# Early weights for the first three ConvFFN units, and one page of w_o a block, in a decoder-layer kernel

## The chip, the cores and the metric

The kernel runs on one core of a Trainium2 chip (one launch, no other core busy). The metric is the device time of that core in microseconds (us), the median over several runs. Five engines are named as in the profile: PE is TensorE (PEld its weight loads), DVE is VectorE, ACT is ScalarE, POOL is GpSimd, SP is SyncE, which here only issues DMAs. Each engine runs its own instructions strictly in the order in which they stand; an instruction that has to wait holds up all that stands behind it on its engine.

## The reference, cut to what matters

The layer takes x (1024 rows of 1024 channels). Three token mixers (stick-breaking attention, mLSTM, cross-attention) and their gates come first and are not touched. What matters here is the end of the merge, the output projection, and the ConvFFN:

```
merged = (gates[:, :, 0] * (y_sb @ w_sb_out[l])
          + gates[:, :, 1] * (y_ml @ w_ml_out[l])
          + gates[:, :, 2] * (y_xa @ w_xa_out[l]))
x = x + merged @ w_o[l]

h = _rmsnorm(x, g_ffn[l])
u = _causal_dwconv(h @ w_up[l], ff_conv_w[l], ff_conv_b[l])
u_val, u_gate = jnp.split(u, 2, axis=-1)
x = x + (jax.nn.silu(u_gate) * u_val) @ w_down[l]
```

w_up is 1024 x 5632: 22 tiles of 128 columns for u_val and 22 for u_gate. All is float32.

## The kernel before, in words

**A matmul is three passes.** Every float32 operand is split into a rounded part and a rest: ACT copies the rounded part (L129), DVE subtracts it from the value (L130). `mm3` (L141 to L144) then multiplies part by part: L142 rounded by rounded, L143 rounded weight by rest of the input, L144 rest of the weight by rounded input.

**Large products have seven parts in place of eight.** Two row halves (l, u) by two halves of the inner dimension (a, b) by two column tiles are computed with seven products of sums and differences (Strassen's scheme in Winograd's form). The output projection does it in seven stages (`stage`, L1224, called from L1235 on); the sums of w_o's pages that it needs are made by `wo_sums` (L1086), a generator stepped once a block (L1141 calls `next(beside)`) while the branches' output projections run, in the last 16 of those 24 blocks. It loads eight pages of 512 KB, two a step, and then does one DVE operation a step (L1096).

**A ConvFFN unit** (`seven`, L698) makes one column tile f of u_val and one of u_gate. Its weights are four quarters: a1, b1 (u_val, first and second half of the inner dimension) and a2, b2 (u_gate). It needs s1 = a2 + b2, a difference a1 - a2, s2 = s1 - a1 (`sums`, L691: DVE operations L694, L695, L696) and b1 - s2 (L727). Its products, 12 matmuls each, are: a1 by "au" and b1 by "bu" (first stage), s2 by "t2" and the difference by "t3" (second stage), s1 by "t1" (third), b1 - s2 by "bl" and b2 by "t4" (fourth). A `yield` ends each stage; the code at the end of the projection steps three units (`first`) by hand and then the others in turn. Inputs au and bu (rows' upper half) are there first; t2 and t3, t1, bl and t4 depend on the norm of the lower half and are split later by ACT and DVE (L1204, L1357, L1366, L1372 and L129, L130).

**Weights of a product** go through two rings, whi and wlo, of two buffers each, so a buffer is free when the product before the last one has been done. `qring` splits a loaded quarter (ACT, DVE). `qadd`, used for the raw quarters a1, b1, b2 of units 0 to 3, spares DVE: ACT makes the rounded part (L671) and its negative (L672), and a DMA issued by POOL adds the weight from DRAM to the negative (L673).

**Order.** A scheduler places the instructions of each engine when the program is built, from the code's order, priorities (`tc.high_priority`) and its own model of times. Before the change only unit 0's weights (L1272 to L1276) are loaded, summed and (a1 alone) split beside the projection's fifth stage. Units 1 and 2 load theirs inside `seven`; their sums stand in DVE's order after the first stages of all three units.

Of the kernel before, what the change touches and what calls it, by code (L numbers as in the profile page):

```python
# [28 lines left out]
NF = DFF // P  # L29
# [13 lines left out]
def tile_hybrid_layer(ctx: ExitStack, tc: tile.TileContext, xT, memT, vecs, w_t, w_n, w_kv, w_if,  # L43
# [4 lines left out]
    nc = tc.nc  # L48
# [19 lines left out]
    def T(shape, tag, dt=F32, bufs=None):  # L68
        pool = {"mw": mlp, "mst": mlp, "px": late[0], "sx": late[0]}.get(tag, sb)
        return pool.tile(shape, dt, tag=tag, name=nm(tag), bufs=bufs or BUFS[tag])  # L70
# [4 lines left out]
    def half(dt=F32):  # L75
        return T([P, HALF], "hf", dt)

    def wide():
        return T([P, S], "U")
# [22 lines left out]
    def hs(h):  # L102
        return slice(h * HALF, (h + 1) * HALF)

    def ts(t):
        return slice(t * P, (t + 1) * P)
# [19 lines left out]
    SOON, LEAD = 40, 60  # L126

    def split(src, hi, lo, eng=None):
        nc.scalar.activation(hi, src, AF.Copy)  # L129
        (eng or nc.vector).tensor_sub(lo, src, hi.bitcast(F32))  # L130
# [10 lines left out]
    def mm3(out, lh, ll, rh, rl, start, stop, more=False):  # L141
        nc.tensor.matmul(out, lh, rh, start=start, stop=False, skip_group_check=more)  # L142
        nc.tensor.matmul(out, lh, rl, start=False, stop=False, skip_group_check=more)  # L143
        return nc.tensor.matmul(out, ll, rh, start=False, stop=stop, skip_group_check=more)  # L144
# [317 lines left out]
    R = NCH * MLH  # L462
# [69 lines left out]
    early = []  # L532
    for b in range(2):
        raw = T([P, S], "y")
# [3 lines left out]
    first = chunks((1,))  # L538
# [110 lines left out]
    RAWS = [itertools.chain(("raw", "raw", "pg"), itertools.repeat("raw")), itertools.repeat("pg")]  # L649

    def turn(i, tags):
        cyc[i] += 1
        return tags[cyc[i] % len(tags)]

    def pair(tag):
        t = T([P, 2, HALF], tag, F32R)
        return t[:, 0], t[:, 1]
# [4 lines left out]
    def qring(src, soon=SOON):  # L662
        t = pair(turn(0, ("whi", "wlo")))
        with tc.high_priority(offset=soon):
            split(src, *t)
        return t

    def qadd(src, dram, soon=SOON):
        t = pair(turn(0, ("whi", "wlo")))
        with tc.high_priority(offset=soon):  # L670
            nc.scalar.activation(t[0], src, AF.Copy)  # L671
            nc.scalar.activation(t[1], t[0].bitcast(F32), AF.Copy, scale=-1.0)  # L672
            nc.gpsimd.dma_start(t[1], dram, accum_op=ALU.add)  # L673
        return t

    def prod(p, a, b, start=True):
        for k in range(4):
            mm3(p, a[0][:, ts(k)], a[1][:, ts(k)], *b[k], start and k == 0, k == 3, not start)

    def halves(src, tag):  # L680

        if tag == "me":
            t = [T([P, HALF], tag) for _ in range(2)]
            for i in range(2):
                nc.sync.dma_start(t[i], src[:, hs(i)])
            return t
        r = T([P, S], tag)
        nc.sync.dma_start(r, src)
        return r[:, hs(0)], r[:, hs(1)]

    def sums(w, s1, s2):  # L691

        a1, b1, a2, b2 = w
        nc.vector.tensor_add(s1, a2, b2)  # L694
        nc.vector.tensor_sub(a2, a1, a2)  # L695
        nc.vector.tensor_sub(s2, s1, a1)  # L696

    def seven(w1, w2, x, done, ready=None, adds=False, pause=False):  # L698

        def raw(src, w, i):  # L700
            return qadd(src, w[:, hs(i)], LEAD) if adds else qring(src)

        w, s1, s2, hl1 = ready or ((*halves(w1, next(RAWS[0])), *halves(w2, next(RAWS[1]))), None, None, None)
        a1, b1, a2, b2 = w
        L, p2 = bank(turn(2, LONG)), bank(turn(3, SHORT))
        prod(L, hl1 or raw(a1, w1, 0), x["au"])
        c1 = wide()
        up, lo = c1[:, hs(1)], c1[:, hs(0)]
        nc.scalar.activation(up, L, AF.Copy)
        if pause:  # L710
            yield
        prod(p2, raw(b1, w1, 1), x["bu"])
        nc.vector.tensor_add(up, up, p2)
        if not ready:
            s1, s2 = half(), a1
            sums(w, s1, s2)
        yield
        prod(L, qring(s2, 1000 if ready else SOON), x["t2"], False)
        c2 = wide()
        nc.scalar.activation(c2[:, hs(1)], L, AF.Copy)  # L720
        R = bank(turn(3, SHORT))
        prod(R, qring(a2, 1000 if ready else SOON), x["t3"])
        yield
        prod(L, qring(s1), x["t1"], False)
        nc.scalar.activation(c2[:, hs(0)], L, AF.Copy)
        nc.vector.tensor_add(c2[:, hs(0)], c2[:, hs(0)], R)
        nc.vector.tensor_sub(b1, b1, s2)  # L727
        yield
        prod(L, qring(b1), x["bl"], False)
        nc.scalar.activation(lo, L, AF.Copy)  # L730
        done(0, c1)
        prod(R, raw(b2, w2, 1), x["t4"], False)
        nc.vector.tensor_add(c2[:, hs(1)], c2[:, hs(1)], R)  # L733
        done(1, c2)
        yield

    def middle(u):
        next(u)
        next(u)
# [338 lines left out]
    def wo_load(q, i, j, tag):  # L1078
        t = T([P, S], tag)
        n = 4 * i + 2 * j  # L1080
        nc.sync.dma_start(t.rearrange("p (n c) -> p n c", n=2), w_o[n:n + 2, :, hs(q)].rearrange("n p c -> p n c"))
        return t
# [3 lines left out]
    def wo_sums():  # L1086
        raw = []
        for j in range(2):
            for qi in (((0, 0), (0, 1)), ((1, 1), (1, 0))):
                raw += [wo_load(q, i, j, "pg") for q, i in qi]  # L1090
                yield
        for j in range(2):
            a1, a2, b2, b1 = raw[4 * j:4 * j + 4]
            for i, op, out, x, y in ((2, nc.vector.tensor_sub, a2, a1, a2), (1, nc.vector.tensor_sub, b2, b2, a2),
                                     (0, nc.vector.tensor_add, a1, a1, b2), (3, nc.vector.tensor_sub, b1, b1, b2)):
                op(out, x, y)  # L1096
                ws[i][j] = out
                yield

    def fine(src, *tags):  # L1100
        t = [T([P, S], tag, F32R) for tag in (tags[0], tags[-1])]
# [13 lines left out]
    w1 = []  # L1115
    beside = wo_sums()
    for i in range(3 * KT):
        b, n = i // KT, ORDER[i % KT]
        if n == 0:
            ys = [branch(b, j) for j in range(4)]  # L1120
        if n < 4:
            raw = T([P, S], "raw")
# [4 lines left out]
        for h in (1, 0):  # L1127
# [4 lines left out]
            dst, t = block(n, h), th[:, hs(h)]  # L1132
# [50 lines left out]
    def grow(o, banks, d):  # L1183
        nc.vector.scalar_tensor_tensor(part(o, d), banks[d], 0.5, part(o, d), op0=ALU.mult, op1=ALU.add)
# [29 lines left out]
    L, R = four(SHORT), four(LONG)  # L1214
# [33 lines left out]
    R = four(LONG)  # L1248
# [23 lines left out]
    w = (*halves(w_up[0], "me"), *halves(w_up[NF], "h"))  # L1272
    early = w, T([P, HALF], "sx"), wide()[:, :HALF]
    sums(*early)
    early += (pair("U"),)
    split(w[0], *early[3])  # L1276

    o1l = out_tiles(0, 0, "y")
    diff = [page("h") for _ in range(2)]
# [6 lines left out]
    def after6(d):  # L1286
        if d == 1:
            with tc.issue_after(last[0].ins):
                upper["r"] = rstd(acc[1], HALF)
        if d == 3:  # L1290
            with tc.issue_after(last[0].ins):
                pr = spread(upper["r"], 4)
            upper["rows"] = half()
            nc.scalar.activation(upper["rows"], pr, AF.Copy)
        grow(o2l, L, d)
        squares(0, part(o2l, d))
        nc.scalar.activation(part(blg, d), part(o2l, d), AF.Copy, scale=col(C_GFFN + 4 + d))
        if d % 2:
            keep(o2l, 1, 0, d // 2)
# [22 lines left out]
    def ffn_up(f):  # L1322
        ys = {}

        def done(g, c):
            i = g * NF + f
            ys[g] = y = T([P, S], "y")
            conv(c, [col(C_FW + 3 * i + 2 - s) for s in range(3)], col(C_FB + i), y)
            if g:
                nc.scalar.activation(y, y, AF.Silu)  # L1330
                nc.vector.tensor_mul(ys[0], ys[0], y)
                if f // 2 == 5:
                    nc.sync.dma_start(act_d[5, f % 2], ys[0])
                else:
                    nc.sync.dma_start(act_d[f // 2, :, :, hs(f % 2)].rearrange("h p r -> p h r"),
                                      ys[0].rearrange("p (h r) -> p h r", h=2))

        return seven(w_up[f], w_up[NF + f], fx, done, early if f == 0 else None, f < 4, f < 3)


    fd, fx = {}, {"au": bau, "bu": bbu}
    for n, tags in (("t2", ("h",)), ("t3", ("pg",)), ("t1", ("h",)), ("bl", ("pg",)), ("t4", ("h", "pg"))):
        fd[n], fx[n] = doubles(*tags)
    units = [ffn_up(f) for f in range(NF)]
    first = units[:3]
    cyc[2], cyc[3] = 1, 1
    next(first[0])
# [6 lines left out]
    with tc.high_priority(offset=300):  # L1354
# [3 lines left out]
            split(full[j], *fd["t2"][j])  # L1358
        for j in range(2):
            split(diff[j], *fd["t3"][j])  # L1360
    for u in first[:2]:
        next(u)
    for j in range(2):
        bl = x1p[2 + j]
# [7 lines left out]
        nc.vector.tensor_sub(full[2 + j], full[2 + j], full[j])  # L1372
        split(full[2 + j], *fd["t4"][j])
    next(first[0])
    middle(first[2])
    next(first[1])
    last = first[2]
    for u in units[3:]:
# [70 lines left out]
    R = [bank(turn(2, LONG)) for _ in range(4)]  # L1449
    L = [bank(turn(3, SHORT)) for _ in range(4)]  # L1450
    au, al, bu, bl, wc = [], [], [], [], []
# [167 lines left out]
```

## Time and profile before

| | |
|---|---|
| runs | 1638.05 us median of 3 (1635.67 to 1638.61) |
| the profiled execution | 1639.59 us; span from first to last instruction 1637.9 us |
| granted TensorE clock, mean | 0.998 |
| PE busy | 99% of the span, 7959 matmuls |
| DVE, ACT, POOL busy | 75%, 51%, 6% |
| DMA | mean 131 GB/s |

The lists of rows below and in the prediction come from this profile. In a timeline row the columns are start (us), duration, engine, line, operation, output<-inputs, shapes, how many were merged, and in brackets the idle time before it with what ended it. A busy PE is not a PE at its peak, since matmuls are pipelined: one starts 0.23 us after the one before it and lasts 0.39 us. What tells is a larger step between starts. The branches' output projections end near 917 us, the output projection of w_o runs to 994 us, and the ConvFFN's units start there.

### The profile page before, as it was taken

The page shows a single profiled execution, that of the slowest core. Times are in us where ns is not written, and L with a number is a line of the kernel's source. Part 1 is how long each engine was busy: PE and PEld are TensorE (multiplying, and loading weights), DVE is VectorE, ACT ScalarE, POOL GpSimd, SP SyncE. Part 2 cuts the span into 40 slices and gives each one's busy share as a digit, 9 for nine tenths or more (in the row PEclk, how much of TensorE's full clock was granted, in tenths as well). Part 3 has the DMA queues.
Part 4 walks back from the last instruction along what each step waited for, and adds up shares of the span by engine and source line. Part 5 has one row for each costly group of instructions (what it writes and reads, how often), then busy time and mean ns, then how long its engine had stood idle before and what let it go on. Part 6 is the DMA issues. An engine that isn't in the chain of part 4 may idle for free.

```text
span 1637.9 us, 21193 instructions
## 1 busy us (share of the span) xinstructions
PE 1617.3 (99%) x7959; PEld 1322.9 (81%) x7959; DVE 1225.8 (75%) x1674; ACT 835.1 (51%) x1281; POOL 104.4 (6%) x175
## 2 busy tenths in 40 slices
PE   8999999999999999999999999999999999999999
PEld 4878888888878888888778887788888888888887
DVE  5658888859774776776576979987787777789864
ACT  4557777645554544666311445655555545543431
POOL 1022222020000110100000001100000000000000
PEclk9999999999999999999999999999999999999999
DMA  8420111324324565434884324431222221577131
GB/s 295 159 66 20 40 40 65 142 95 151 128 99 154 192 191 158 140 111 155 310 293 147 117 97 109 129 103 71 77 82 99 91 78 52 186 303 244 46 135 71
DMA packets 101794, 214.54 MB, mean 131 GB/s; under 512 B 13304, under 2 KB 37176, under 8 KB 101692
## 3 DMA queue, kind: packets, MB, share of 16 engines
q1 hardware_dynamic: 100108, 210.30, 37.0%
q0 software_dynamic: 1584, 2.88, 1.1%
q8 instruction: 63, 1.03, 0.3%
q14 instruction: 39, 0.32, 0.1%
HBM read 158.54 MB, written 54.61 MB: 130 GB/s over the span
## 4 chain that ended last, share of the span: by engine, by line
PE 93%; DMA 2%; DVE 2%; ACT 2%; issue 1%; POOL 0%; SPq 0%; DVEq 0%; ACTq 0%; POOLq 0%
PE ps_pj L142 13%; PE ps_pj L144 13%; PE ps_pj L143 13%; PE ps_pv L144 6%; PE ps_pv L142 6%; PE ps_pv L143 6%; PE ps_tr L142 4%; PE ps_tr L143 4%; PE ps_tr L144 4%; PE ps_z L142 4%; PE ps_z L144 4%; PE ps_z L143 4%; PE ps_pv L440 2%; PE ps_tr L420 2%; PE ps_z L395 1%; PE ps_z L394 1%
## 5 line engine op out<-in xcount | busy, mean ns | idle before, releaser
L143 PE MATMUL ps_pj<-h,whi 128*128 128x512 f32 x520 | 204.1, 393 | 0.0
L142 PE MATMUL ps_pj<-h,whi 128*128 128x512 f32 x440 | 176.4, 401 | 4.0 <-ACT h L129 2.7
L129 ACT ACTIVATE whi<-raw 128x512 fp32r<-128x512 f32 (+1 forms) x99 | 81.2, 821 | 168.7 <-PE ps_pj L143 76.5
L144 PE MATMUL ps_pj<-h,wlo 128*128 128x512 f32 x352 | 137.4, 390 | 0.1
L842 DVE SCALAR_TENSOR_TENSOR y<-U,vec,y 128x1023 f32<-128x1023 f32 x88 | 112.4, 1279 | 8.1 <-ACT y L840 8.1
L143 PEld LDWEIGHTS ps_pj<-h,whi 128*128 128x128 f32 x520 | 98.3, 189 | 20.0 <-DVE h L130 0.8
L408 DVE TENSOR_TENSOR_SCAN U<-U 128x512 f32<-128x512 f32 (+3 forms) x96 | 92.8, 1008 | 22.0 <-POOL U L403 20.4
L142 PE MATMUL ps_pj<-pg,whi 128*128 128x512 f32 x268 | 104.7, 391 | 1.3 <-DVE pg L1134 1.3
L142 PEld LDWEIGHTS ps_pj<-h,whi 128*128 128x128 f32 x440 | 83.2, 189 | 21.8 <-ACT h L129 3.4
L144 PE MATMUL ps_pj<-pg,wlo 128*128 128x512 f32 x248 | 96.7, 390 | 0.0
L144 PEld LDWEIGHTS ps_pj<-h,wlo 128*128 128x128 f32 x352 | 66.1, 188 | 14.7 <-DVE wlo L130 0.6
L129 ACT ACTIVATE whi<-pg 128x512 fp32r<-128x512 f32 (+1 forms) x53 | 43.1, 815 | 66.2 <-PE ps_tr L143 18.3
L143 PE MATMUL ps_pv<-h,whi 128*128 128x512 f32 x190 | 74.0, 389 | 0.0
L143 PE MATMUL ps_pj<-pg,whi 128*128 128x512 f32 x188 | 73.4, 390 | 0.0
L130 DVE TENSOR_TENSOR wlo<-raw,whi 128x1024 fp32r<-128x1024 f32 x44 | 53.7, 1221 | 17.3 <-ACT whi L129 17.3
L840 ACT ACTIVATE y<-U,vec 128x1024 f32<-128x1024 f32 x44 | 54.6, 1242 | 20.6 <-DVE U L733 16.8
L144 PE MATMUL ps_pj<-h,whi 128*128 128x512 f32 x160 | 63.3, 396 | 0.0
L142 PEld LDWEIGHTS ps_pj<-pg,whi 128*128 128x128 f32 x268 | 50.3, 188 | 12.0 <-DVE pg L1134 1.9
L144 PE MATMUL ps_pv<-h,wlo 128*128 128x512 f32 x152 | 59.6, 392 | 0.0
L142 PE MATMUL ps_pv<-h,whi 128*128 128x512 f32 x150 | 58.9, 393 | 0.3 <-DVE U L733 0.3
L130 DVE TENSOR_TENSOR wlo<-raw,wlo 128x512 fp32r<-128x512 f32 x53 | 36.5, 688 | 26.6 <-ACT wlo L129 26.3
L144 PE MATMUL ps_tr<-pg,wlo 128*128 128x512 f32 x144 | 56.0, 389 | 0.0
(489 smaller groups left out, 4478.1 us busy)
## 6 DMA issues: line engine op xcount, KB each, us to landing
raw<-in_w_t_dram SPq DMA_DIRECT2D x29, 512.0 KB
gate_d<-U SPq DMA_DIRECT2D x24, 512.0 KB
U<-gate_d SPq DMA_DIRECT2D x22, 512.0 KB
act_d<-y SPq DMA_DIRECT2D x22, 512.0 KB
pg<-in_w_t_dram SPq DMA_DIRECT2D x21, 512.0 KB
raw<-in_w_dn_dram SPq DMA_DIRECT2D x18, 512.0 KB
h<-act_d SPq DMA_DIRECT2D x14, 512.0 KB
raw<-in_w_br_dram SPq DMA_DIRECT2D x12, 512.0 KB
```

Source lines behind the costliest of these rows:

```text
L129: nc.scalar.activation(hi, src, AF.Copy)
L130: (eng or nc.vector).tensor_sub(lo, src, hi.bitcast(F32))
L142: nc.tensor.matmul(out, lh, rh, start=start, stop=False, skip_group_check=more)
L143: nc.tensor.matmul(out, lh, rl, start=False, stop=False, skip_group_check=more)
L144: return nc.tensor.matmul(out, ll, rh, start=False, stop=stop, skip_group_check=more)
L394: nc.tensor.matmul(z[:, a, :w], qs[a][:, ts(rb)], ks[a][:, c], start=True, stop=False)
L395: nc.tensor.matmul(z[:, a, :w], qs[a][:, ts(rb)], kz[a][:, c], start=False, stop=True)
L408: nc.vector.tensor_tensor_scan(f[:, a, 1:w + 1], f[:, a, 1:w + 1], f[:, a, 1:w + 1], 1.0 if o == 0 else f[:, a, 0:1], op0=ALU.mult, op1=AL ...
L420: nc.tensor.transpose(pt[:, a, ts(j)], g[:, a, ts(j)], ident)
L440: nc.tensor.matmul(pv[64 * a:64 * a + 64, ts(rb % 4)], sbv[s // 2][:, s % 2, (2 * p + a) * 64:(2 * p + a + 1) * 64], wt[a][:, ts(j)], star ...
L840: nc.scalar.activation(out, u, AF.Identity, bias=bias, scale=taps[0])
L842: nc.vector.scalar_tensor_tensor(out[:, :S - s], u[:, s:], taps[s], out[:, :S - s], op0=ALU.mult, op1=ALU.add)
```

## The change

Four things change, all between about 820 and 1065 us:

1. The weights of units 1 and 2 are loaded beside the projection's fifth stage, with unit 0's; their first two sums are made in place in the projection's sixth stage (s1 in b2's place, the difference in a2's), one operation after each of its four column tiles. s2 is made later, in a1's place. So b2 is overwritten, and is loaded a second time (256 KB each, `if s1 is b2`) for the fourth stage.
2. Unit 0's s2 and difference are split there too, into a pair each of the five "U" buffers.
3. Unit 2's second stage is stepped together with those of units 0 and 1, ahead of unit 0's third; before, it came after unit 0's fourth.
4. `wo_sums` loads one page a block in place of two; the subtraction a2 = a1 - a2 shares its step with the operation after it.

```
-        w, s1, s2, hl1 = ready or ((*halves(w1, next(RAWS[0])), *halves(w2, next(RAWS[1]))), None, None, None)
+        w, s1, s2, pre = ready or ((*halves(w1, next(RAWS[0])), *halves(w2, next(RAWS[1]))), None, None, {})
...
-        if not ready:
+        if s1 is None:
             s1, s2 = half(), a1
             sums(w, s1, s2)
+        elif s2 is None:
+            s2 = a1
+            nc.vector.tensor_sub(s2, s1, a1)
...
-        prod(L, qring(s2, 1000 if ready else SOON), x["t2"], False)
+        prod(L, pre.get("s2") or qring(s2), x["t2"], False)
...
+        if s1 is b2:
+            b2 = half()
+            nc.sync.dma_start(b2, w2[:, hs(1)])
...
-            for qi in (((0, 0), (0, 1)), ((1, 1), (1, 0))):
-                raw += [wo_load(q, i, j, "pg") for q, i in qi]
+            for q, i in ((0, 0), (0, 1), (1, 1), (1, 0)):
+                raw.append(wo_load(q, i, j, "pg"))
                 yield
...
+    soon = []
+    for f, tag in ((1, "h"), (2, "pg")):
+        w = (*halves(w_up[f], "raw"), *halves(w_up[NF + f], tag))
+        soon.append((w, w[3], None, {}))
...
+        a1, b1, a2, b2 = soon[d // 2][0]
+        if d % 2 == 0:
+            nc.vector.tensor_add(b2, b2, a2)
+        else:
+            nc.vector.tensor_sub(a2, a1, a2)
...
-    for u in first[:2]:
+    for u in first:
         next(u)
...
     next(first[0])
-    middle(first[2])
+    next(first[2])
     next(first[1])
```

The built order on the engines changes as follows; outside of this stretch it is the same. (Numbers behind a name tell tiles apart; the changed kernel has other line numbers, so L713, L726 and L727 there stand for the same as before or six lines lower.)

**DVE, at the second stages.** First what stood before. raw_8708 and h_8710 are unit 1's weights, raw_8739 and pg_8741 unit 2's; L713 adds up first-stage results; L1204 scales the rows behind "t1", "bl" and "t4", L1366 forms t1.

```order
L713 TENSOR_TENSOR U_8730<-U_8730,ps_z_8713 128x512
L694 TENSOR_TENSOR hf_8797<-h_8710 128x512
L713 TENSOR_TENSOR U_8761<-U_8761,ps_pv_8744 128x512
L695 TENSOR_TENSOR h_8710<-raw_8708,h_8710 128x512
L694 TENSOR_TENSOR hf_8818<-pg_8741 128x512
L696 TENSOR_TENSOR raw_8708<-hf_8797,raw_8708 128x512
L695 TENSOR_TENSOR pg_8741<-raw_8739,pg_8741 128x512
L130 TENSOR_TENSOR wlo_8885<-h_8710,wlo_8885 128x512
L130 TENSOR_TENSOR whi_8867<-raw_8708,whi_8867 128x512
L696 TENSOR_TENSOR raw_8739<-hf_8818,raw_8739 128x512
L130 TENSOR_TENSOR whi_8908<-sx_8462,whi_8908 128x512
L130 TENSOR_TENSOR wlo_8926<-hf_8797,wlo_8926 128x512
```

And now (unit 1: raw_8476, h_8478; unit 2: raw_8480, pg_8482; L1211 is the old L1204, L1385 the old L1366):

```order
L713 TENSOR_TENSOR U_8744<-U_8744,ps_z_8727 128x512
L130 TENSOR_TENSOR whi_8865<-raw_8476,whi_8865 128x512
L130 TENSOR_TENSOR wlo_8883<-h_8478,wlo_8883 128x512
L713 TENSOR_TENSOR U_8771<-U_8771,ps_pv_8754 128x512
L130 TENSOR_TENSOR whi_8898<-raw_8480,whi_8898 128x512
L130 TENSOR_TENSOR wlo_8916<-pg_8482,wlo_8916 128x512
L1211 TENSOR_TENSOR pg_8206<-pg_8206,ps_tr_8751 128x1024
L1211 TENSOR_TENSOR pg_8207<-pg_8207,ps_tr_8751 128x1024
L1385 TENSOR_TENSOR y_8484<-pg_8206,pg_8202 128x1024
```

The six sums are gone from this place: four stand some 45 rows earlier (L1309 and L1311, in the projection's sixth stage), the two that form s2 (L719) some ten rows earlier. Two splits of unit 0's weights have also gone up.

**SP, at the branches' last third.** Before:

```order
L1177 DMA px_8132<-in_xT_dram 128x2x512
L1081 DMA pg_7439<-in_w_o_dram 128x2x512
L1081 DMA pg_7441<-in_w_o_dram 128x2x512
L1081 DMA pg_7475<-in_w_o_dram 128x2x512
L1081 DMA pg_7477<-in_w_o_dram 128x2x512
L1068 DMA U_7515<-gate_d 128x1024
L1081 DMA pg_7517<-in_w_o_dram 128x2x512
L1081 DMA pg_7519<-in_w_o_dram 128x2x512
```

And now:

```order
L1184 DMA px_8132<-in_xT_dram 128x2x512
L1087 DMA pg_7439<-in_w_o_dram 128x2x512
L1087 DMA pg_7473<-in_w_o_dram 128x2x512
L1074 DMA U_7511<-gate_d 128x1024
L1087 DMA pg_7513<-in_w_o_dram 128x2x512
L1087 DMA pg_7547<-in_w_o_dram 128x2x512
L1087 DMA pg_7587<-in_w_o_dram 128x2x512
L1074 DMA U_7545<-gate_d 128x1024
```

The third page of w_o now stands behind a gate page. On DVE the first sum needs pages one and two, the second page three; before, both stood in a row (L1096, L1096); now the rows that empty a PSUM bank and use it (L1143, L1144) stand between them, and the second and third sums stand in a row.

**DVE, beside the projection's sixth stage.** Before:

```order
L696 TENSOR_TENSOR U_8463<-sx_8462,me_8456 128x512
L130 TENSOR_TENSOR U_8467<-me_8456,U_8467 128x512
L1200 TENSOR_TENSOR hf_8031<-hf_8031,hf_8383 128x512
L1184 SCALAR_TENSOR_TENSOR U_8280<-ps_pj_8209,U_8280 128x512
L130 TENSOR_TENSOR wlo_8399<-pg_7439,whi_8398 128x1024
```

And now:

```order
L696 TENSOR_TENSOR U_8463<-sx_8462,me_8456 128x512
L1309 TENSOR_TENSOR h_8478<-h_8478 128x512
L1207 TENSOR_TENSOR hf_8031<-hf_8031,hf_8383 128x512
L1191 SCALAR_TENSOR_TENSOR U_8280<-ps_pj_8209,U_8280 128x512
L130 TENSOR_TENSOR U_8467<-me_8456,U_8467 128x512
L130 TENSOR_TENSOR wlo_8399<-pg_7439,whi_8398 128x1024
```

The first of the four sums has come in; the other three follow in the same way up to the projection's second column tile of that stage.

**PE** changes only within 192 rows, from unit 0's second stage on. The products of 12 matmuls stand there in this order (unit, operand; in brackets those that are interleaved):

```
before: 0 t2, 0 t3, (1 t3 with 1 t2), 0 t1 and 1 t1, (0 bl, 0 t4, 2 t2), 2 t3, (1 bl with 2 t1), 1 t4, 3 au, 3 bu, 2 bl, 2 t4
after:  (0 t2 with 0 t3), 1 t2, 1 t3, 2 t2, 2 t3, 0 t1, 1 t1, 0 bl, 0 t4, 1 bl, (1 t4 with 2 t1), 3 au, (3 bu with 2 bl), 2 t4
```

Before, 36 matmuls stood between the last use of the buffer into which unit 1's b2 (for its "t4") goes and the first use of that b2; after the change, 24 do.

More of the change, by code (lines that the diff above doesn't have):

```diff
@@ L701, in raw @@
             return qadd(src, w[:, hs(i)], LEAD) if adds else qring(src)
-        w, s1, s2, hl1 = ready or ((*halves(w1, next(RAWS[0])), *halves(w2, next(RAWS[1]))), None, None, None)
+        w, s1, s2, pre = ready or ((*halves(w1, next(RAWS[0])), *halves(w2, next(RAWS[1]))), None, None, {})
         a1, b1, a2, b2 = w
         L, p2 = bank(turn(2, LONG)), bank(turn(3, SHORT))
-        prod(L, hl1 or raw(a1, w1, 0), x["au"])
+        prod(L, pre.get("a1") or raw(a1, w1, 0), x["au"])
         c1 = wide()
@@ L721, in seven @@
         R = bank(turn(3, SHORT))
-        prod(R, qring(a2, 1000 if ready else SOON), x["t3"])
+        prod(R, pre.get("a2") or qring(a2), x["t3"])
         yield
+        if s1 is b2:
+            b2 = half()
+            nc.sync.dma_start(b2, w2[:, hs(1)])
         prod(L, qring(s1), x["t1"], False)
@@ L1097, in wo_sums @@
                 ws[i][j] = out
-                yield
+                if i != 2:
+                    yield
     def fine(src, *tags):
@@ L1274, in tile_hybrid_layer @@
     sums(*early)
-    early += (pair("U"),)
-    split(w[0], *early[3])
+    early += ({n: pair("U") for n in ("a1", "s2", "a2")},)
+    for n, t in (("a1", w[0]), ("s2", early[2]), ("a2", w[2])):
+        split(t, *early[3][n])
+    soon = []
+    for f, tag in ((1, "h"), (2, "pg")):
+        w = (*halves(w_up[f], "raw"), *halves(w_up[NF + f], tag))
+        soon.append((w, w[3], None, {}))
     o1l = out_tiles(0, 0, "y")
@@ L1336, in done @@
                                       ys[0].rearrange("p (h r) -> p h r", h=2))
-        return seven(w_up[f], w_up[NF + f], fx, done, early if f == 0 else None, f < 4, f < 3)
+        return seven(w_up[f], w_up[NF + f], fx, done, (early, *soon)[f] if f < 3 else None, f < 4, f < 3)
     fd, fx = {}, {"au": bau, "bu": bbu}
@@ L1344, in tile_hybrid_layer @@
     units = [ffn_up(f) for f in range(NF)]
+    for _ in range(2):
+        next(RAWS[0]), next(RAWS[1])
     first = units[:3]
```

## The prediction

> **What bounds the kernel now.** I read the page first, then TensorE's waits over the whole run, then the stretch where the longest of the late ones lies.
>
> ```profile
> span 1637.9 us, 21193 instructions
> PE 1617.3 (99%) x7959; PEld 1322.9 (81%) x7959; DVE 1225.8 (75%) x1674; ACT 835.1 (51%) x1281; POOL 104.4 (6%) x175
> ```
> ```profile
> PE ps_z L215 <- ACT pg L185: 6.7, 1, 6.7
> PE ps_pj L142 <- ACT h L129: 2.7, 1, 2.7
> PE ps_pj L142 <- DVE U L1136: 1.3, 1, 1.3
> PE ps_pj L142 <- DVE pg L1134: 1.3, 1, 1.3
> ```
>
> TensorE is the bound; only its waits and its clock can be won. The 6.7 us are at the start. Two rows lie where the change works: 2.7 us before the units' "t1" product, and 1.3 us in the branches' projections (L1136). How much the first costs in all is seen in stretches of equal length, the second undisturbed:
>
> ```profile
> core 0: us, PE busy (x) PEld busy (x) DVE busy (x) ACT busy (x) POOL busy (x), PEclk, DMA share, GB/s
> 1012.68:1036.78 24.10, 20.57 (x74) 15.10 (x72) 22.28 (x28) 10.51 (x16) 0.86 (x1) 0.86 0.16 44
> 1080.00:1104.10 24.10, 24.10 (x108) 19.96 (x107) 17.83 (x25) 11.67 (x18) 0.00 (x0) 1.00 0.33 105
> 1027.92:1034.03 6.11, 6.07 (x13) 4.29 (x14) 5.21 (x5) 0.89 (x1) 0.16 (x1) 0.50 0.64 172
> ```
> ```profile
> 1009.96 0.39 PE L142 MATMUL ps_pv<-h,wlo 128*128 128x512 f32 x1
> ...
> 1012.68 0.39 PE L142 MATMUL ps_pj<-h,whi 128*128 128x512 f32 x1
> ```
>
> A product of 12 takes 1012.68 - 1009.96 = 2.72 us, 0.227 a matmul. In the stalled stretch 108 - 74 = 34 matmuls are missing: 34 x 0.227 = 7.7 us. So the 2.7 us row is a third of it. Right behind it TensorE ran 6.11 us at clock 0.50, in which 13 matmuls started that need 2.95 us: 3.2 us lost by the clock. The rest are small waits ahead of the stall.
>
> Why it stalled, from VectorE's timeline and ScalarE's:
>
> ```profile
> 1014.82 0.68 DVE L713 TENSOR_TENSOR U<-U,ps_pv 128x512 f32<-128x512 f32 x1
> 1015.42 0.68 DVE L713 TENSOR_TENSOR U<-U,ps_z 128x512 f32<-128x512 f32 x1
> 1016.01 0.68 DVE L694 TENSOR_TENSOR hf<-h 128x512 f32<-128x512 f32 x1
> ...
> 1022.64 2.34 DVE L1204 TENSOR_TENSOR pg<-pg,ps_tr 128x1024 f32<-128x1024 f32 x2
> 1024.90 2.35 DVE L1366 TENSOR_TENSOR y<-pg,pg 128x1024 f32<-128x1024 f32 x2
> ```
> ```profile
> 1026.82 1.99 ACT L129 ACTIVATE h<-y 128x1024 fp32r<-128x1024 f32 x2
> ```
> ```profile
> 1024.84 0.39 PE L144 MATMUL ps_pv<-pg,wlo 128*128 128x512 f32 x1
> 1027.92 0.79 PE L142 MATMUL ps_pj<-h,whi 128*128 128x512 f32 x1 [2.69 <-ACT h L129]
> ```
>
> VectorE works without a pause there, 0.60 us from start to start at 512 columns (1015.42 to 1016.01) and 1.13 at 1024 (2.26 for two, 1022.64 to 1024.90). The units' sums (L694 on) stand ahead of L1204 and L1366, whose result ScalarE splits for "t1". VectorE's order, not its load over the run, makes the stall.
>
> **The stall, after the change.** I walk the new order with these durations.
> - The six sums are gone from between L713 and L1204; two (the s2's, 1.2 us) now stand about ten rows earlier, and unit 0's two splits (1.2) have gone up altogether. In the same stretch unit 0's b1 - s2 (0.6) has moved behind.
> - With these, the L713 rows start near 1014.0 in place of 1014.82, the L1204 pair at 1018.2 in place of 1022.64, the first L1366 at 1020.5. The first half of "t1" is split by 1024.7, the second by 1026.6.
> - TensorE in the meantime has two products more ahead of "t1" (unit 2's second stage): six from 1012.68, so it asks for "t1" at 1012.68 + 6 x 2.72 = 1029.0. The splits are 2.4 us early even for the last of them. ScalarE's waits for ring buffers (a product earlier each time) are in the walk and leave it ahead.
>
> So the whole 7.7 us go: the idle, the half clock behind it, and the small waits, whose splits (of units 1 and 2) now also come 2 us before use.
>
> **Where the sums went.** Four sums (2.4 us) and two splits (1.2) now lie at 965 to 976. VectorE's pauses there:
>
> ```profile
> 962.65 0.69 DVE L694 TENSOR_TENSOR sx<-h 128x512 f32<-128x512 f32 x1 [0.67 <-DMA h<-in_w_up_dram]
> ...
> 970.11 0.69 DVE L1200 TENSOR_TENSOR hf<-hf,hf 128x512 f32<-128x512 f32 x1 [0.70 <-ACT hf L1199]
> ...
> 976.21 0.69 DVE L1184 SCALAR_TENSOR_TENSOR px<-ps_pv,px 128x512 f32<-128x512 f32 x1 [2.03 <-PE ps_pv L144]
> ```
>
> The walk has VectorE up to 1.2 us late at 974 and level again at 977; the weights it splits there are wanted about 3 us later. Cost nothing, and 1 us for each us if the cover went.
>
> The sums wait for pages. SyncE's issues before:
>
> ```profile
> 958.30 0.35 SPq L688 DMA_DIRECT2D h<-in_w_up_dram  x1
> 962.01 0.33 SPq L688 DMA_DIRECT2D raw<-in_w_up_dram  x1
> 965.89 0.33 SPq L685 DMA_DIRECT2D me<-in_w_up_dram  x1
> 967.10 4.77 SPq L1188 DMA_DIRECT2D x_d<-U  x2
> ```
>
> The page issued at 958.30 was in use at 962.65, 4.35 us later. Unit 1's second page goes right behind it (958.7) and is wanted at 965.2; unit 2's goes behind the first L1188 and one L685 (968.3) and is wanted at 975.3: 7 us. Both fit. Behind a late one on VectorE would stand the statistics of the norm, which TensorE wants at 983. The second load of b2 (two of 256 KB) is issued near 996, in place of a page; nobody wants it before 1037. Cost nothing.
>
> **The new wait.** Unit 1's b2 goes through the adding DMA. Its chain before:
>
> ```profile
> 1046.44 0.62 ACT L671 ACTIVATE whi<-h 128x512 fp32r<-128x512 f32 x1
> 1047.10 0.63 ACT L672 ACTIVATE whi<-whi 128x512 fp32r<-128x512 f32 x1
> ```
> ```profile
> 1048.03 0.86 POOL L673 DMA_DIRECT2D whi<-in_w_up_dram  x1 [19.95 <-PE ps_z L144]
> ```
> ```profile
> DMA to landing us min/median/max: 3.6/6.2/7.2
> ```
>
> L671 to the issue takes 1.6 us, 1.9 with another ScalarE operation between (there is one now), and some 0.4 from TensorE's release. Landing takes L = 3.6 to 7.2. Before, 36 matmuls lay between the buffer's release and its use; now 24, and the third matmul of the product is the first that needs the added part: 27 x 0.227 = 6.1 us after the last matmul that used the buffer. The wait is 2.3 + L - 6.1 = L - 3.8: nought to 3.4 us. Three pages are loaded just ahead of it, so I take L from the upper half, a little under the median: 5.7, and 1.9 us. Behind, unit 3's b1 has 30 matmuls (L - 4.4) and more time once TensorE has waited; unit 2's b2 and unit 0's b2 are within half a microsecond, as unit 1's and 2's were before. Together 2.0 us, bounds 0 and 5.
>
> [...] No adding DMA in this trace landed in under 3.6.
>
> **The pages of w_o.**
>
> ```profile
> 825.19 1.97 SPq L1081 DMA_DIRECT2D pg<-in_w_o_dram  x4
> 830.09 0.34 SPq L1068 DMA_DIRECT2D U<-gate_d  x1
> ```
> ```profile
> 833.94 2.57 DVE L1096 TENSOR_TENSOR pg<-pg,pg 128x1024 f32<-128x1024 f32 x2 [1.42 <-DMA pg<-in_w_o_dram]
> 836.42 0.68 DVE L1136 SCALAR_TENSOR_TENSOR U<-U,ps_pj 128x512 f32<-128x512 f32 x1
> ```
> ```profile
> 837.16 0.50 PE L142 MATMUL ps_pj<-h,whi 128*128 128x512 f32 x1 [1.31 <-DVE U L1136]
> ```
>
> VectorE waited for the second page, did two sums, and only then L1136, which frees TensorE's bank. Now one sum stands ahead of that row: if the page still lands at 833.9, L1136 starts at 835.1 and TensorE at 835.8, so 1.3 us come back. But the third page is now issued behind the gate page, at 830.5. The second page took 8.2 us from 825.7 to use; the third has less ahead of it and I put it at 836.5. Then two sums in a row delay the next bank by 1.0 us. Net gain 0.3; bounds 1.3 gained and, if it also takes 8.2 us (838.7), 3.2 - 1.3 = 1.9 lost and a half clock behind it (3.2).
>
> **Sum.** Gains 7.7 + 0.3, loss 2.0: 6.0 us. Made against the profiled execution (1639.59 us, span 1637.9) that is 1633.6; the median of the runs, 1638.05, is 1.5 lower, so 1632.0.
>
> **Rivals.**
> - *The adding DMAs land early* (3.6 us): no new wait, gain 8.0, 1630.0. For: two before landed that soon, with nothing loaded around them. Against: three pages go ahead now. 0.15.
> - *The new wait halves the clock.* The 2.69 us idle did, the 1.3 us did not; in between no row tells. From L = 6.5 the wait is 2.7 us: 0.8 more than summed, and 3.2 for the clock: 1636.0. For: the median is 6.2. 0.13. [...]
> - *Another late step takes the stall's place*: VectorE is as late as before at another split, gain 1 us, 1637.0. Against: the walk has 2.4 us to spare. 0.06.
> - *Slower: single pages of w_o hold VectorE in block after block.* Place: the four sums that now stand behind a page issued alone (third, sixth, seventh, eighth). It decides from a landing 8 us after issue, as the second page's was: 1.9 us lost at the third page, 2 at each of the others, twice 3.2 for the clock, 14.3 against 7.7 - 2.0 = 5.7 gained: 8.6 slower, 1646.6. Against: less is queued ahead of each than ahead of the second page. 0.06.
> - Forecast: 0.60, its own range 1629 to 1635.
>
> **Numbers.** No change that a measurement can tell is within 0.2%, 3.3 us: 1634.8 to 1641.3. Faster: 0.57 of the forecast, 0.15, and a little of the clock rival: 0.73. Same: the rest of these and the third rival: 0.21. Slower: 0.06. The range goes from the early landing less the runs' spread to the third rival: 1628.5 to 1637.0.
>
> **What would show it.** In the changed profile: no TensorE wait over 1 us between 1010 and 1037 and clock 1.00 there; VectorE's L1204 pair near 1018; a TensorE wait for an adding DMA about 30 us after unit 0's second stage starts; the wait at 837 smaller or one product later. I am wrong if the 2.7 us wait and the clock 0.50 are still in that stretch, if VectorE waits for an in_w_up page near 965 to 976 by over 2 us, or if the branches' stretch lost more than it did.

## The result, and the profile after

| | before | changed |
|---|---|---|
| median, 20 runs each | 1639.24 us (1635.67 to 1642.98) | 1634.67 us (1632.30 to 1638.45) |
| ratio | | 0.9973, 95% interval 0.9965 to 0.9980 |
| profiled execution | 1639.59, span 1637.9 | 1633.01, span 1631.3 |

The median fell by 4.6 us, the profiled execution by 6.6; 6.0 was forecast. One execution of those reported below, of the early sums alone (2), took 2314.81 us at a mean granted clock of 0.655 and is left out of its ratio. The head of the page after the change:

```profile
span 1631.3 us, 21183 instructions
PE 1613.9 (99%) x7959; PEld 1322.4 (81%) x7959; DVE 1226.2 (75%) x1674; ACT 835.5 (51%) x1281; POOL 103.6 (6%) x175
```

VectorE is as busy as before (1226 us): nothing was saved, work was moved. TensorE's waits after the change (us in total, how often, the longest):

```profile
PE ps_pv L144 <- DMA whi<-in_w_up_dram: 2.1, 1, 2.1
...
PE ps_pj L142 <- DVE U L1143: 0.5, 1, 0.5
```

The 2.7 us row and the two of 1.3 us are gone; there is a new one of 2.1 us on an adding DMA. In stretches, first before, then after:

```profile
786.00:860.00 74.00, 71.41 (x313) 57.97 (x312) 48.63 (x59) 15.13 (x15) 0.00 (x0) 1.00 0.86 301
...
1036.78:1065.00 28.22, 28.22 (x124) 22.64 (x122) 26.81 (x33) 20.37 (x30) 3.45 (x4) 1.00 0.55 150
```
```profile
786.00:860.00 74.00, 73.41 (x322) 59.98 (x321) 51.16 (x62) 15.23 (x15) 0.00 (x0) 1.00 0.90 311
1012.68:1036.78 24.10, 24.10 (x108) 19.74 (x106) 23.80 (x29) 13.10 (x19) 0.86 (x1) 1.00 0.27 74
1036.78:1065.00 28.22, 26.09 (x114) 20.96 (x114) 24.94 (x32) 20.34 (x29) 3.44 (x4) 1.00 0.53 140
```

Read the first bracket, TensorE's matmuls in stretches of equal length. From 1012.68 to 1036.78 there are 108 in place of 74, as many as in the undisturbed stretch, at clock 1.00: 34 x 0.227 = 7.7 us won. From 1036.78 on there are 10 fewer: 2.3 us lost. In the branches 9 more: 2.0 us. Together these would make 7.4 us, 0.8 more than the 6.6 us by which the span fell; 2 matmuls fewer in the first 100 us, 3 fewer from there to 786 us and differences of one elsewhere make the rest. Whether the 2.0 us belong to the change is the first question for the experiments.

The walk of VectorE and ScalarE to "t1", which ended at the old stall:

```profile
1017.57 2.35 DVE L1211 TENSOR_TENSOR pg<-pg,ps_tr 128x1024 f32<-128x1024 f32 x2
1019.83 1.22 DVE L1385 TENSOR_TENSOR y<-pg,pg 128x1024 f32<-128x1024 f32 x1
```
```profile
1021.08 1.06 ACT L129 ACTIVATE h<-y 128x1024 fp32r<-128x1024 f32 x1 [0.18 <-DVE y L1385]
...
1023.52 1.05 ACT L129 ACTIVATE h<-y 128x1024 fp32r<-128x1024 f32 x1
```
```profile
1028.17 0.39 PE L142 MATMUL ps_pj<-h,whi 128*128 128x512 f32 x1
```

The rounded halves of "t1" are there at 1022.1 and 1024.6, TensorE takes the first at 1028.17 with no wait (there is no bracket). The forecast had 1024.7, 1026.6 and 1029.0.

The new wait, on ScalarE, on GpSimd (with the time from issue to landing of this one DMA) and on TensorE:

```profile
1036.53 0.63 ACT L671 ACTIVATE whi<-hf 128x512 fp32r<-128x512 f32 x1 [1.60 <-PE ps_pj L144]
...
1037.54 0.62 ACT L672 ACTIVATE whi<-whi 128x512 fp32r<-128x512 f32 x1
```
```profile
1038.45 0.86 POOL L673 DMA_DIRECT2D whi<-in_w_up_dram  x1 [6.76 <-ACT whi L672]
```
```profile
DMA to landing us min/median/max: 6.0/6.0/6.0
```
```profile
1044.46 0.50 PE L144 MATMUL ps_pv<-h,whi 128*128 128x512 f32 x1 [2.06 <-DMA whi<-in_w_up_dram]
```

It is the row that was forecast: unit 1's b2, at the third matmul of its product, 1.92 us from L671 to the issue (1.9 forecast), 6.0 to land (5.7), 2.06 us of wait (1.9).

The sums of w_o:

```profile
833.27 1.23 DVE L1102 TENSOR_TENSOR pg<-pg,pg 128x1024 f32<-128x1024 f32 x1 [0.84 <-DMA pg<-in_w_o_dram]
...
835.79 2.49 DVE L1102 TENSOR_TENSOR pg<-pg,pg 128x1024 f32<-128x1024 f32 x2
...
850.16 1.23 DVE L1102 TENSOR_TENSOR pg<-pg,pg 128x1024 f32<-128x1024 f32 x1 [0.53 <-DMA pg<-in_w_o_dram]
```

One sum stands ahead of the row that frees TensorE's bank, then two in a row, and TensorE loses 0.5 us one product later. For the pages loaded singly VectorE waited 0.53 us at most later on in this profile.

### The profile page after: what moved, and what is told of

Read it like the earlier page. It is cut to its first block, busy times and chain, and to the rows that moved or that the text cites. A ratio compares the mean times of both kernels' runs of the same rounds, so it can differ in the third digit from the quotient of the medians.

```text
span 1631.3 us, 21183 instructions
## 1 busy us (share of the span) xinstructions
PE 1613.9 (99%) x7959; PEld 1322.4 (81%) x7959; DVE 1226.2 (75%) x1674; ACT 835.5 (51%) x1281; POOL 103.6 (6%) x175
## 4 chain that ended last, share of the span: by engine, by line
PE 92%; DMA 3%; DVE 3%; ACT 1%; issue 1%; SPq 0%; POOL 0%; DVEq 0%; ACTq 0%
PE ps_pj L142 13%; PE ps_pj L144 13%; PE ps_pj L143 13%; PE ps_pv L144 5%; PE ps_pv L142 5%; PE ps_pv L143 5%; PE ps_z L142 4%; PE ps_z L144 4%; PE ps_z L143 4%; PE ps_tr L142 4%; PE ps_tr L143 4%; PE ps_tr L144 4%; PE ps_pv L440 2%; PE ps_tr L420 2%; PE ps_z L215 1%; PE ps_z L395 1%
## 5 line engine op out<-in xcount | busy, mean ns | idle before, releaser
L143 PE MATMUL ps_pj<-h,whi 128*128 128x512 f32 x516 | 201.7, 391 | 0.0
L142 PE MATMUL ps_pj<-h,whi 128*128 128x512 f32 x436 | 173.9, 399 | 0.6 <-DVE U L1143 0.5
L144 PE MATMUL ps_pj<-h,whi 128*128 128x512 f32 x156 | 60.8, 390 | 0.0
```

## The experiments

Every ratio is against the kernel before, timed in turn with it on the same chip (its medians there 1638.88, 1638.98 and 1639.59 us in the three series), from 5 to 12 executions of each kernel.

**1. The pages alone, and the change without them.**

```diff
 (before, w_o's pages one a block)
-            for qi in (((0, 0), (0, 1)), ((1, 1), (1, 0))):
-                raw += [wo_load(q, i, j, "pg") for q, i in qi]
+            for q, i in ((0, 0), (0, 1), (1, 1), (1, 0)):
+                raw.append(wo_load(q, i, j, "pg"))
                 yield
...
-                yield
+                if i != 2:
+                    yield
```

> Before, with one page of w_o loaded a block and nothing else changed. Theory (the pages are a small term of the change): the wait at the branches' projections goes from 1.3 to about 0.5 us as in the changed kernel, the 2.7 us wait before t1 and the half clock behind it stay, and the time falls by 0.8 us, which the runs can't tell from nothing (0.999 to 1.0005). Rival (the pages carry a good part of the gain, by what they take off the DMA engines): 2 us or more (below 0.9988). Rival (single pages hold VectorE): slower, with waits of 2 us at the sums of the later pages.

The other way round, in the changed kernel the same lines were put back:

> The changed kernel with w_o's pages loaded two a block as before. Theory: the 1.3 us wait at the branches' projections is back, the stretch from 1012 to 1037 us stays clean, and the new wait of 2.1 us stays: 0.8 us more than the changed kernel, about 0.9978 of before. Rival (the pages carry a good part): 2 us or more above the changed kernel, 0.9985 or higher.

Measured: the pages alone 1639.3 us, ratio 1.0001 (0.9992 to 1.0010); the change without them 1633.6 us, 0.9967 (0.9955 to 0.9979). TensorE's waits with the pages alone:

```profile
PE ps_pj L142 <- ACT h L129: 2.7, 1, 2.7
...
PE ps_pj L142 <- ACT whi L129: 0.9, 1, 0.9
...
PE ps_pj L142 <- DVE pg L1135: 0.5, 1, 0.5
```

The old stall is there as before. In the branches the longest wait for VectorE is 0.5 in place of 1.3 us, the longest of all 0.9 us, for a split by ScalarE; in the change without the pages the wait for the row that frees TensorE's bank is back, at 1.5 us. Yet the time does not tell. (Over all profiles of this document the longest wait for that row is 0.2 to 1.2 us in ten with single pages, 0.9 to 1.5 in three with pairs.) The reason is in the matmul counts between 786 and 860 us, where the DMA engines are busy at 0.86 to 0.90: before 313, pages alone 315, changed 322, changed without the pages 318; but two more profiles of the changed kernel as it is (3, below) have 305 and 316. Executions of the same code differ there by 17 matmuls, 3.9 us. So the 2.0 us that the first profile showed in this stretch are not shown to be the change's, and neither theory's 0.8 us nor nothing can be told apart. A part of 2 us or more is ruled out.

**2. The new order alone, and the early sums alone.** The change has two ways to keep TensorE from the stall: two products more ahead of "t1", and six sums fewer ahead of L1204. First only the order, in the kernel before:

```diff
-    for u in first[:2]:
+    for u in first:
         next(u)
...
-    middle(first[2])
+    next(first[2])
```

> Before, with unit 2's second stage stepped ahead of unit 0's third, and nothing else changed: TensorE has two products (5.4 us) more ahead of t1, and VectorE makes the six sums where they were. Theory (VectorE's order makes the stall; it is late by less than two products): TensorE asks for t1 at about 1029, and its first half is split near 1028 to 1030: a wait of 0 to 1.5 us, no half clock, and the new wait for unit 1's b2 as in the changed kernel, since its cover is shortened by the order: 4 us less than before (0.9975). Rival (the early sums are what counts; without them unit 2's own sums and splits come too late for its second stage): the stall only moves to unit 2's products, 2 to 3 us idle and a half clock: within 1 us of before (0.9995 to 1.0005).

Measured: 1643.8 us, ratio 1.0021 (1.0011 to 1.0031): slower than before, which neither theory had. Its waits, the stretch behind the stall's place, and the adding DMA for unit 1's b2 with its landing:

```profile
PE ps_pv L144 <- DMA whi<-in_w_up_dram: 4.9, 1, 4.9
PE ps_z L144 <- DMA whi<-in_w_up_dram: 2.1, 1, 2.1
```
```profile
1012.68:1036.78 24.10, 23.30 (x102) 18.50 (x101) 24.10 (x31) 14.06 (x21) 0.86 (x1) 1.00 0.18 44
1036.78:1065.00 28.22, 23.33 (x90) 18.55 (x89) 19.89 (x25) 15.05 (x23) 3.44 (x4) 0.88 0.49 134
```
```profile
1041.79 0.86 POOL L673 DMA_DIRECT2D whi<-in_w_up_dram  x1 [9.45 <-ACT whi L672]
```
```profile
DMA to landing us min/median/max: 7.3/7.3/7.3
```

The theory holds for the stall (102 matmuls, clock 1.00, no wait over 0.5 us there) and fails on the price of the new wait. The prediction's formula, 2.3 + L - cover, gives it after the fact: the products are interleaved otherwise here, 20 matmuls or 4.5 us lie between release and use, and L was 7.3, behind three pages of 512 KB issued from 1039.8 to 1041.3. That makes 5.1; the row says 4.9. Two waits (7.0) and half clock behind both (3.4 and 1.7) cost more than the old stall's 7.7.

Then the changed kernel with only the order put back:

```diff
-    for u in first:
+    for u in first[:2]:
         next(u)
...
-    next(first[2])
+    middle(first[2])
```

> The changed kernel with unit 2's second stage in its old place, after unit 0's fourth: the sums are made early, TensorE has no more products ahead of t1 than before. Theory: without the sums VectorE has t1 ready at about 1021 to 1023 and TensorE asks at 1023.6: no wait over 0.5 us and clock 1.00; and 36 matmuls again cover unit 1's b2, so the new wait is gone too: 2 us less than the changed kernel, about 0.996 of before. Rival (both parts are needed): a wait of 1 to 3 us before t1 is back, with or without the half clock behind it: 0.9985 to 1.0 of before.

Measured: 1634.3 us, ratio 0.9968 (0.9956 to 0.9981), the same as the whole change. A wait and the stretches:

```profile
PE ps_tr L142 <- ACT U L723: 1.0, 1, 1.0
...
PE ps_pv L144 <- DMA whi<-in_w_up_dram: 0.3, 1, 0.3
```
```profile
1012.68:1036.78 24.10, 23.00 (x98) 17.82 (x97) 23.46 (x28) 12.23 (x17) 0.86 (x1) 1.00 0.21 65
1036.78:1065.00 28.22, 27.95 (x122) 22.56 (x122) 27.17 (x34) 21.42 (x30) 3.45 (x4) 1.00 0.59 150
```

As the theory had it, the new wait is gone (0.3). It was wrong that nothing would be lost ahead of it: 98 matmuls, 10 fewer than the 108 of a clean stretch, 2.3 us. The longest wait there, 1.0 us, is not for "t1" but for ScalarE's copy that empties a product's bank (L723). So the early sums, with unit 0's two early splits that belong to the same edit and were not timed apart, bring the gain without the new order, and unit 2's new place only exchanges one loss of 2.3 us for another.

**3. The changed kernel again, twice.** No edit.

> The changed kernel once more, to be the measure for the three others of this series and to give a second profile. Theory: 4 to 6 us less than before (0.9965 to 0.9975); the one wait between 1010 and 1065 is that for unit 1's b2, 1.5 to 2.5 us. Rival (the gain of the median is smaller than that of the first profile because the new wait is often longer and then halves the clock): this profile or others of the kernel show clock 0.50 near 1045.

> The changed kernel a third time, as the measure of this series, with a third profile. Two profiles of it showed the new wait at 2.06 us with clock 1.00 behind it and at 2.45 us with half clock behind it. Theory (whether about 2 to 2.7 us idle halves the clock is a matter of where it falls, not of its length alone): wait 1.5 to 2.7 us, the clock either way. Rival (a threshold between 2.06 and 2.45): half clock exactly where the wait is over some 2.1 us. 0.9965 to 0.9975 of before.

Measured: 1632.9 us, 0.9970 (0.9958 to 0.9981), and 1633.0 us, 0.9964 (0.9951 to 0.9978). The first of the two profiles is of an execution of 1638.11 us:

```profile
PE ps_pv L144 <- DMA whi<-in_w_up_dram: 2.5, 1, 2.5
```
```profile
1036.78:1065.00 28.22, 25.77 (x107) 20.73 (x106) 23.14 (x29) 18.23 (x27) 3.45 (x4) 0.94 0.59 153
```

Half clock follows the wait here (0.94, 107 matmuls in place of 114: 1.6 us more, of which 0.4 is the longer wait). In the other the wait is 1.97 us at clock 1.00. So the same code shows the rival of the halved clock in some executions and not in others. This execution is 5.1 us longer than the first profile's; its 305 matmuls in the branches, 17 fewer, are 3.9 us of that, and the longer wait with its half clock is 1.6, together a little more than all of it.

**4. A longer wait.** In the changed kernel, for unit 1's b2 alone:

```diff
             nc.scalar.activation(t[1], t[0].bitcast(F32), AF.Copy, scale=-1.0)
+            for _ in range(more):
+                nc.scalar.activation(t[1], t[0].bitcast(F32), AF.Copy, scale=-1.0)
             nc.gpsimd.dma_start(t[1], dram, accum_op=ALU.add)
```

> The changed kernel with ScalarE's negative of unit 1's b2 made three times in place of once ahead of its adding DMA (the same values again; 1.0 to 1.2 us later). Two matmuls of unit 3 come ahead of the product's third in TensorE's order, so the wait grows from 2.1 to 2.6 to 2.9 us. Theory A (about 2.7 us idle is enough to halve the clock, as before the change): clock 0.50 for some 6.8 us behind it, 0.7 + 3.3 = 4 us more than the changed kernel. [...]

Measured: 1633.5 us, 0.9964 (0.9951 to 0.9977). The wait did not grow:

```profile
1041.40 0.86 POOL L675 DMA_DIRECT2D whi<-in_w_up_dram  x1 [9.46 <-ACT whi L674]
```
```profile
DMA to landing us min/median/max: 4.0/4.0/4.0
```
```profile
1045.42 0.71 PE L144 MATMUL ps_pv<-h,whi 128*128 128x512 f32 x1 [2.10 <-DMA whi<-in_w_up_dram]
```

Issued 3 us later than in the changed kernel's first profile, and 4 us after the last page ahead of it, the DMA landed in 4.0 us in place of 6.0, which took back what the later issue had cost. Half clock followed all the same (0.83 over the ten microseconds behind it). So it came behind a shorter wait, 2.10 us, than Theory A's 2.7; the length of the wait alone does not order what the profiles show (last section).

**5. Is it the pages ahead of the adding DMA?** The raw and page loads of units 6 and 7 are held back. Of the three pages of 512 KB that went ahead of unit 1's b2 in the changed kernel this stops two; one (issued at 1036.09) still goes ahead:

```diff
+        if hold:
+            with tc.issue_after(add[0].ins):
+                nc.gpsimd.memset(r[:, :2], 0.0)
         nc.sync.dma_start(r, src)
```

> The changed kernel with the raw and page loads of units 6 and 7 held back until the last adding DMA (unit 3's) has been issued, by a two-column write that GpSimd puts into their tiles behind it. They are first wanted after 1105. Theory (the pages loaded just ahead make the adding DMA's landing long): unit 1's b2 lands in 4 to 5 us after issue in place of 6.0, the wait goes from 2.1 to 0 to 1 us: 1.5 us less than the changed kernel. Rival (the landing is long whatever is queued): still 5.5 to 6.5 us to land and a wait of 1.5 to 2.5, no gain.

Measured: 1634.4 us, 0.9974 (0.9965 to 0.9983), no gain. Unit 1's b2 and TensorE's one wait:

```profile
1039.78 0.86 POOL L673 DMA_DIRECT2D whi<-in_w_up_dram  x1 [6.77 <-ACT whi L672]
...
1051.98 0.86 POOL L673 DMA_DIRECT2D whi<-in_w_up_dram  x1 [8.50 <-PE ps_tr L144]
```
```profile
DMA to landing us min/median/max: 3.7/3.7/3.7
```
```profile
1057.20 0.50 PE L144 MATMUL ps_pv<-h,whi 128*128 128x512 f32 x1 [2.34 <-DMA whi<-in_w_up_dram]
```

The theory is right about the landing: 3.7 us for the DMA issued at 1039.78, and no wait for it. But no time is won, since the next product fed this way, unit 3's b1 (issued at 1051.98, 5.2 us to land), now makes TensorE wait 2.34 us. In the changed kernel it had been covered only because TensorE had waited before. The prediction's formula would give it less than 1 us at this landing (L - 4.4). What it lacks is ScalarE's work ahead of the split, the SiLU of a finished tile and the load of its function table:

```profile
1047.81 1.28 ACT L1352 ACT_TABLE_LOAD   x1 [2.10 <-DVE y L853]
1049.10 1.06 ACT L1352 ACTIVATE y<-y 128x1024 f32<-128x1024 f32 x1
1050.07 0.61 ACT L671 ACTIVATE whi<-px 128x512 fp32r<-128x512 f32 x1
```

The last matmul that used the buffer started at 1047.90, so it took 4.1 us from there to the issue, in place of 2.3. With 30 matmuls (6.8 us) to the first use that makes 4.1 + 5.2 - 6.8 = 2.5 us; the row says 2.34.

**6. Unit 1's and 2's b2 by the engines.**

```diff
+        again = s1 is b2
-        if s1 is b2:
+        if again:
...
-        prod(R, raw(b2, w2, 1), x["t4"], False)
+        prod(R, qring(b2) if again else raw(b2, w2, 1), x["t4"], False)
```

> The changed kernel with the second b2 of units 1 and 2 split by ScalarE and VectorE, as the sums are, in place of the adding DMA. Theory (the adding DMA's chain, 2.3 us plus its landing, is longer than its cover): the split is ready some 1.9 us after the buffer's release against a cover of 6, no wait near 1042, two VectorE operations (1.2 us) more that nobody waits for: 2 us less than the changed kernel, about 0.996 of before. Rival (VectorE has no room there; its work comes late instead): a wait of 1 us or more for VectorE between 1040 and 1065, no gain over the changed kernel.

Measured: 1635.5 us, 0.9976 (0.9966 to 0.9986), no gain, but not for the rival's reason: TensorE waits for VectorE nowhere between 1010 and 1100. The wait has gone to the same place as in 5 (ScalarE's SiLU and table load stand between L671 and L672 here, and the landing takes 5.0 us):

```profile
1057.47 0.50 PE L144 MATMUL ps_pv<-h,whi 128*128 128x512 f32 x1 [2.57 <-DMA whi<-in_w_up_dram]
```

**7. No adding DMA behind unit 0's.** Unit 3's quarters are also split by the engines:

```diff
-        return seven(w_up[f], w_up[NF + f], fx, done, (early, *soon)[f] if f < 3 else None, f < 4, f < 3)
+        return seven(w_up[f], w_up[NF + f], fx, done, (early, *soon)[f] if f < 3 else None, f < 3, f < 3)
```

> The changed kernel with the second b2 of units 1 and 2 and unit 3's a1, b1, b2 split by ScalarE and VectorE in place of the adding DMA; those of units 0 to 2 that remain are a1, b1 and unit 0's b2. Theory (splitting unit 1's b2 alone only handed the wait on to the next product fed by an adding DMA, unit 3's b1): with none left behind unit 0's, no TensorE wait over 0.5 us between 1010 and 1100 and clock 1.00; 2.3 to 2.6 us less than the changed kernel (0.9955 of before). Rival (VectorE can't take five splits more, 3 us, between 1035 and 1090): waits of over 1 us for VectorE's splits or sums in that stretch, no gain over the changed kernel.

And with unit 0's b2 (every `raw(b2, w2, 1)` is `qring(b2)`):

> As ring_all, with unit 0's b2 split on the engines too, so that only the a1 and b1 of units 0 to 2 go through adding DMAs. Theory: within 0.5 us of ring_all, since unit 0's b2 made TensorE wait 0 to 0.5 us. Rival: one split more on VectorE near 1030, where t1, bl and t4 are made ready, delays those: a wait for an h or pg operand there, 1 us or more above ring_all.

Measured: 1631.6 us, 0.9951 (0.9939 to 0.9963), and 1630.1 us, 0.9950 (0.9937 to 0.9962), against 0.9964 (0.9951 to 0.9978) for the changed kernel in the same series. The second one's stretch behind the stall's place:

```profile
1036.78:1065.00 28.22, 28.22 (x126) 23.36 (x125) 28.22 (x36) 19.61 (x27) 0.00 (x0) 1.00 0.30 108
```

126 matmuls in place of 114 (125 in the first one), and no wait over 0.3 us from 1010 to 1100 in either. VectorE is busy all through it (28.22 of 28.22 us) and yet not waited for. This is the fastest version: 0.5% below the kernel before. Below the changed kernel of the same series the medians are 1.4 us (forecast 2.3 to 2.6) and 2.9 us. With five executions each the intervals overlap with the change's, so the times alone do not show the gain; the stretches do. The two versions can't be told apart (0.9951 and 0.9950).

## Why the prediction was right

- *The stall.* Right in mechanism and size: forecast 7.7 us, measured 34 matmuls or 7.7 us. That VectorE's order made it, not its load, is shown by experiment 2, where the early sums (with unit 0's splits) take it away without the new order. The size is that of one execution: with the pages alone the same stall left 79 matmuls in the stretch, 29 too few or 6.6 us, since half clock lasted 3.41 us there and 6.83 in the profile that the prediction read.
- *Where the sums went.* Right: nothing waits for them between 965 and 983, and both pages were in time.
- *The new wait.* Forecast 1.9 us at unit 1's b2, measured 2.06 (1.97 and 2.45 in the other profiles), 10 matmuls with the small ones (2.3, forecast 2.0). The reason for the long landing, pages just ahead, is shown by experiment 5: 3.7 us with two of the three held back. The 5.7 itself was a choice; the text calls it the upper half of 3.6 to 7.2 and puts it under the median of 6.2, and the changed kernel's three profiles have 6.0, 6.4 and 6.2.
- *What the step on the wait left out.* The prediction said that unit 3's b1 has more time "once TensorE has waited". That is half of a chain: the waits are one shortage handed on, and to shorten the first alone wins nothing (5, 6). It also took 2.3 us from release to issue for that product too, where ScalarE's SiLU and its table load make it 4.1 (5).
- *The pages.* Forecast 0.3 us, bounds 1.3 and -1.9: too small to be told from the stretch's own spread of 3.9 us. The rival of single pages that hold VectorE fell: VectorE waited 0.53 us at most for any of the later pages in the first profile, and 1.28 at most in the others with single pages (pages alone), not 2 a page.
- *The halved clock.* This rival, 3.2 us from a wait of 2.7 on, was built on the wait's length, which alone does not tell (last section): no half clock came behind 2.34 (5) and 2.57 us (6), 3.41 us of it behind 1.83 (6) and 2.10 (4). Behind the 2.45 us of the changed kernel's second profile it was 3.41 us, half of them or 1.7 us lost, and it comes to some executions of the changed kernel and not to others. It is a part of what the sum lacked, of about 0.7 us on the average at most (last section); the rest is not shown. Forecast 6.0, measured 4.6 in one set of runs and 6.1 and 6.6 in two smaller ones.
- *The level.* The forecast of 1632.0 us stood on a median of three runs, 1638.05; twenty gave 1639.24. The 1634.67 measured lies at the upper end of its own range, 1629 to 1635: the mechanism was right, that the number fell within was close.
- *What was not asked.* That unit 2's second stage might not be needed. The prediction counted its two products as slack ahead of "t1" and its lost cover as a price, and did not set the one against the other.

## What to carry to other kernels

Look at what stands ahead of a late operation on its engine before counting that engine's load; moving sums and splits to a place with pauses won the time here, with VectorE as busy as before. When an order is changed, compute for each transfer that a buffer's release starts (release to issue with what else stands on the engines between, plus landing, less the work between release and use), for all of them in a row: a shortage cured at one is handed to the next. Keep short what waits remain: in the last section's table the one of 1.57 us cost its own length only, and behind seven of the eleven from 1.83 us on TensorE ran at half clock for 3.41 or 6.83 us. Where two edits serve one end, time each alone; here one of them brought the gain without the other, which alone made the kernel slower.

## What the runs showed of the hardware

**Half clock came behind some of TensorE's waits and not behind others, and their length alone does not tell which.** I read the granted clock of every profile in windows of half a microsecond and noted where half clock begins. In the order alone, for example,

```profile
1048.10:1048.60 0.50, 0.00 (x0) 0.00 (x0) 0.50 (x1) 0.00 (x0) 0.00 (x0) 0.73 1.03 192
1048.60:1049.10 0.50, 0.00 (x1) 0.00 (x1) 0.50 (x2) 0.29 (x1) 0.00 (x0) 0.50 0.94 205
```

the mean clock of 0.73 in the first window, ahead of 0.50 in the second, says that the clock fell after 0.23 us, at 1048.33. Every profile has one such place behind its last instruction (in before at 1638.63), and some have others: before at 1027.64, the order alone at 1048.33 and 1068.81, the second profile of the changed kernel at 1049.11. The end of half clock is read in the same way; in the order alone it lasted from 1048.33 to 1055.16, 6.83 us. TensorE's waits and what stood behind them:

| wait, us | execution | half clock behind it, us |
|---|---|---|
| 1.57 | change without the pages | 0 |
| 1.83 | experiment 6, at 820 | 3.41 |
| 1.97 | changed, third profile | 0 |
| 2.06 | changed, first profile | 0 |
| 2.10 | experiment 4 | 3.41 |
| 2.10 | order alone, second | 3.41 |
| 2.34 | held (5) | 0 |
| 2.45 | changed, second profile | 3.41 |
| 2.57 | experiment 6, at 1057 | 0 |
| 2.69 | before | 6.83 |
| 2.69 | pages alone | 3.41 |
| 4.89 | order alone, first | 6.83 |

The length of the wait does not order these rows: behind 2.57 us there was no half clock, behind 1.83 there was, and of the two waits of 2.69 us one had 6.83 us of it and the other 3.41. In the two rows with 6.83 the clock fell while TensorE still waited (0.28 and 0.77 us before the end), in the five with 3.41 it fell after the wait. What sets the rows apart is left open here. The wait of 6.3 to 7.0 us ahead of each execution's first matmul is not in the table. The clock column reads 1.00 there, and yet in before the first eight matmuls took 5.56 us and the next eight of the same kind 3.60, so what the clock was in the first ten microseconds is not shown. The ten microseconds around the end of the wait, for 2.10 us (experiment 4) and for 2.57 us (experiment 6):

```profile
1044.92:1054.92 10.00, 9.50 (x35) 7.70 (x36) 8.42 (x12) 6.55 (x9) 0.86 (x1) 0.83 0.58 147
```
```profile
1056.97:1066.97 10.00, 9.50 (x42) 7.87 (x43) 8.25 (x11) 5.82 (x7) 0.00 (x0) 1.00 0.11 41
```

The longer wait cost no clock, the shorter one 7 matmuls. How often the changed kernel meets half clock has a bound in the runs. Of the 31 timed executions of the changed kernel, in all three sets, 18 have a mean clock of 1.000, and one stretch of 3.41 us at half clock in 1632 us would make it 0.999; so at most 13 of 31, 0.42, had one. Their median is 1635.59 us, that of the 18 others 1633.06. The new wait's price is then at most 2.3 + 0.42 x 1.7 = 3.0 us on the average, where the forecast's 2.0 left the clock out. 7.7 - 3.0 = 4.7 us is near the 4.6 by which the median of the 20 runs fell, but the stall's 7.7 is one execution's, and in the 11 of those 20 with a mean clock of 1.000 the median, 1634.21, is still only 5.0 us below before: the clock does not close the sum.

**The same adding DMA of 256 KB, unit 1's b2, took 3.7 us (experiment 5, two pages held back), 4.0 (4), 6.0 to 6.4 (the change, three profiles) and 7.3 us (the order alone, three pages just ahead)** from issue to landing, so that in these runs its price went with what SyncE had been let loose to load a few microseconds earlier.
